# Output product to feed-forward of a two-layer backbone: VectorE's order written by hand, tiles in another assignment to halves

## The chip, the cores and the metric

The kernel runs on one core of a Trainium2 chip. Its time is the device time of one execution in microseconds; three executions of the kernel before are given, and one further execution was taken with a hardware profile.

## The reference

One inference step of two layers on 1024 sample tokens and 128 prompt tokens of width 1024, in float32. Each layer is a mixer (layer 0: a diagonal state-space scan beside a Fourier mixer; layer 1: pooling beside a gated MLP) and a squared-ReLU feed-forward, each between two RMS norms with a shift, scale and gate computed from the condition:

```python
def rmsnorm(x, g):
    xf = x.astype(F32)
    y = xf * lax.rsqrt(jnp.mean(xf * xf, axis=-1, keepdims=True) + EPS)
    return (y * g.astype(F32)).astype(x.dtype)

def run_layer(x, cond, mixer, ...):
    sh1, sc1, gt1, sh2, sc2, gt2 = modulation(cond, w_mod, b_mod)
    h = rmsnorm(x, g_mix_pre) * (1.0 + sc1) + sh1
    y, aux = mixer(h)                       # its last step is a product with w_out (1024 x 1024)
    x = x + gt1 * rmsnorm(y, g_mix_post)
    h = rmsnorm(x, g_ff_pre) * (1.0 + sc2) + sh2
    x = x + gt2 * rmsnorm(jnp.square(jax.nn.relu(h @ w1)) @ w2, g_ff_post)
```

The stage of this case lies between the mixer's product with w_out and the first product of the feed-forward with w1 (1024 x 4096).

## The kernel before

Tokens lie in nine tiles of 128: tiles 0 to 7 are the sample, tile 8 the prompt. A float32 operand of a product is split into a high and a low part in a rounded format (ScalarE writes the high part with a Copy, VectorE the low part with a subtraction), and each product is three matmuls: high by high, high by low, low by high.

`mixer_out` (L777) makes the product with w_out for one tile and one half of the 512 output columns at a time: `mm_tm` issues 24 matmuls (L252 to L254) into a PSUM bank `po`, of which there are three in turn. The activations of tiles 0 to 2, 3 to 5 and 6 to 8 are groups 0, 1 and 2, in the slots A0 to A15. The order is: first half of tiles 0, 1, 2, second half of the same, then both halves of 3, 8, 4, 5, 6, 7. The weights of the second half lie in W0 to W7. ScalarE copies `po` to `y` (L797; slots Y0, Y1 and E in turn); after a tile's second half `add_normed` (L674) takes the norm (`rms_scales`, L180), multiplies by the gate row `gt` (slot T, L688), adds the residual `xr` loaded by SP (L694), stores the sum, takes the next norm and scales (L699). `raw_tile` (L723) transposes the tile on TensorE (L731) and converts the blocks with scale and shift into the four quarters `raw` of one half j of the tokens (slots R0 to R7): tiles 0 to 3 and half of the prompt are half 0, tiles 4 to 7 half 1. Four of a tile's eight blocks are converted by ScalarE (L746) and four by VectorE (L744); tile 8 takes 32 small steps of ScalarE (L737).

`factors` (L749) then makes, for each half j, the seven right-hand factors x of a fast (seven-product) form of the feed-forward's first product: four sums of quarters (L766 to L773) and seven splits into a high part on ScalarE (L758, L761) and a low part on VectorE (L759, L762). They go to the slots that the table `XQ` lists. Names such as x14l in the profile are half 1, factor 4, low part.

`ff_up` (L808) runs 16 weight pairs. For a pair it makes seven weight factors (L841 on ScalarE, L842 and the sums L850 to L858 on VectorE), runs seven products of 12 matmuls a half (L96 to L98, 288 columns, in the banks puA, puB, puC) and turns them into hidden blocks (L893 to L915). The first pair runs half 0 through all seven products (1, 2, 6, 5, 7, 3, 4) and then half 1; the others run both halves product by product. In layer 0, jobs that compute modulation vectors (L126, with weights `mst` loaded to slot E and to staging slots) follow the pairs one by one.

The program's text gives dependencies and a priority; the order on each engine is set at build time by a planner that issues, engine by engine, what its model holds ready, earlier text first. `tc.manual_schedule(engines=...)` keeps the instructions of the named engines in the order of the text; the kernel before uses it for SP's DMA queue in the first stage.

The last stage (`ff_down`, L958) finishes tiles with the same `add_normed`, in layer 1 in the order 2, 3, 6, 7, 8, 0, 1, 4, 5; `layer1_mixer` (L1125) gates its three groups in the order 0, 1, 2.

Of the kernel before, what the change touches and what calls it, by code (L numbers as in the profile page):

```python
# [9 lines left out]
F32 = mybir.dt.float32  # L10
# [169 lines left out]
def rms_scales(K, ys):  # L180

    nc, v = K.nc, K.nc.vector
    n = len(ys)
    t = K.small.tile([128, 6, 3], F32, name="rms", tag="rms", bufs=4)
    for i, y in enumerate(ys):
        junk = K.small.tile([128, D], BF16, name="junk", tag="junk", bufs=1)
        nc.scalar.activation(junk, y, AF.Square, accum_out=t[:, 0, i:i + 1])
    t = t[:, :, :n]
    v.tensor_scalar(t[:, 1], t[:, 0], 1.0 / D, EPS, op0=ALU.mult, op1=ALU.add)
    nc.scalar.activation(t[:, 2], t[:, 1], AF.Sqrt)  # L190
    v.reciprocal(t[:, 3], t[:, 2])
    v.tensor_tensor(t[:, 4], t[:, 3], t[:, 3], op=ALU.mult)
    v.tensor_tensor(t[:, 4], t[:, 4], t[:, 1], op=ALU.mult)
    v.tensor_scalar(t[:, 4], t[:, 4], -0.5, 1.5, op0=ALU.mult, op1=ALU.add)
    v.tensor_tensor(t[:, 5], t[:, 3], t[:, 4], op=ALU.mult)
# [61 lines left out]
def build(tc, A):  # L257
# [6 lines left out]
    with ExitStack() as top:  # L264
# [20 lines left out]
        K.csil = csil  # L285
        K.xs = tc.dram_tile([D, D], F32, name="xs")
# [423 lines left out]


XQ = {}
for _ks, _ns in (([(j, i, p) for i in (1, 2) for j in (0, 1) for p in "hl"], [f"A{n}" for n in range(8)]),
                 ([(0, 6, "h"), (0, 6, "l"), (1, 6, "h"), (0, 5, "h"), (0, 5, "l"), (0, 7, "h"), (0, 7, "l"), (0, 3, "h")],
                  [f"A{n}" for n in range(8, 16)]),
                 ([(0, 3, "l"), (0, 4, "h"), (0, 4, "l")], ["W0", "W1", "W2"]),
                 ([(1, 6, "l"), (1, 5, "h"), (1, 5, "l")], ["Y0", "Y1", "T"]),
                 ([(1, 7, "h"), (1, 7, "l"), (1, 3, "h"), (1, 3, "l")], ["R0", "R1", "R2", "R3"]),
                 ([(1, 4, "h"), (1, 4, "l")], ["R5", "R7"])):
    XQ.update(zip(_ks, _ns))  # L720


def raw_tile(K, t, y, raw, scale, shift):  # L723
# [3 lines left out]
    v = nc.vector  # L727
    for kh in range(2):
# [3 lines left out]
        for k in range(4):  # L732
            kb = 4 * kh + k
            if t == 8:
                for j in range(2):
                    for b in range(2):
                        nc.scalar.activation(raw[j][2 * kh + b][:, k, 256:288],  # L737
                                             ps[:, 128 * k + 64 * j + 32 * b:128 * k + 64 * j + 32 * b + 32],
# [38 lines left out]
def mixer_out(K, layer, acts):  # L777
# [14 lines left out]
    for t, h in [(t, h) for h in range(2) for t in range(3)] + [(t, h) for t in (3, 8, 4, 5, 6, 7) for h in range(2)]:  # L792
        if h == 0:
            y[t] = yp.tile([128, D], F32, "y")
# [962 lines left out]
```

## Time and profile before

| | us |
|---|---|
| three executions | 2440.43, 2440.82 (median), 2446.5 |
| the profiled execution | 2445.58 |
| span of the profile | 2443.8 |
| TensorE busy (matmul) | 2276.6 (93%) |
| VectorE busy | 1715.2 (70%) |
| ScalarE busy | 986.1 (40%) |
| GpSimd busy | 193.4 (8%) |
| layer 0: output products, then the feed-forward's first pair | 488.3 to 592.5, 592.5 to 655.5 |
| layer 1: end of the output products to the end of the first pair | 1680.6 to 1738.4 |

Times in the rows are microseconds from the start of the span unless marked ns. PE is TensorE (PEld its weight loads), DVE VectorE, ACT ScalarE, POOL GpSimd, SPq the DMA queue that SyncE issues. L694 is line 694 of the kernel. [...]

### The profile page before, as it was taken

How to read it: one execution, taken by the hardware profiler on the slowest of the kernel's cores; microseconds unless marked ns; L12 is line 12 of the kernel's file. 1: busy time of each engine (PE TensorE's matmuls, PEld its weight loads, DVE VectorE, ACT ScalarE, POOL GpSimd, SP SyncE). 2: the span in 40 equal slices, each digit the busy share in tenths (PEclk: the TensorE clock that was granted, in tenths of full speed). 3: DMA queues.
4: the chain of work that ended last, by engine and by line, in shares of the span. 5: the costliest groups of instructions: out<-in, count | busy, mean ns of one | idle time of the engine just before them, and what ended most of it. 6: DMA issues, size and time to landing. Idle time of an engine off the chain costs nothing.

```text
span 2443.8 us, 34950 instructions
## 1 busy us (share of the span) xinstructions
PE 2276.6 (93%) x13462; PEld 1983.6 (81%) x13462; DVE 1715.2 (70%) x2800; ACT 986.1 (40%) x1712; POOL 193.4 (8%) x196
## 2 busy tenths in 40 slices
PE   7997775998799999999999799998899999999996
PEld 4996543987688889988888599887899999888884
DVE  7888998646665555756768944877765567567779
ACT  4543334546332233454333452446433334543332
POOL 0126863200000000000000000000000000000000
PEclk9998887999999999999999899998999999999998
DMA  8375573322456554644433431131344446444334
GB/s 316 132 247 184 187 271 114 128 79 86 135 184 222 183 168 133 234 155 139 127 113 101 170 123 40 61 112 67 115 145 128 131 144 229 149 141 127 122 102 172
DMA packets 200455, 361.50 MB, mean 148 GB/s; under 512 B 50064, under 2 KB 95760, under 8 KB 198240
## 3 DMA queue, kind: packets, MB, share of 16 engines
q1 hardware_dynamic: 200288, 359.26, 44.6%
q8 instruction: 106, 1.74, 0.3%
q14 instruction: 61, 0.50, 0.1%
HBM read 256.69 MB, written 102.51 MB: 147 GB/s over the span
## 4 chain that ended last, share of the span: by engine, by line
PE 76%; DVE 16%; ACT 3%; DMA 2%; issue 2%; POOL 1%; SPq 0%; DVEq 0%; ACTq 0%
PE pz L1060 7%; PE pz L1058 7%; PE pz L1059 7%; PE puA L96 6%; PE puA L97 5%; PE puA L98 5%; DVE tp L1559 3%; PE puC L96 3%; PE puC L98 3%; PE puC L97 3%; PE po L252 2%; PE po L253 2%; PE po L254 2%; PE pmod L126 2%; DVE xp L1566 1%
## 5 line engine op out<-in xcount | busy, mean ns | idle before, releaser
L1060 PE MATMUL pz<-wh,hl 128*128 128x512 f32 x840 | 324.8, 389 | 2.6 <-DVE hl L1053 2.6
L1059 PE MATMUL pz<-wl,hh 128*128 128x512 f32 x840 | 326.8, 389 | 0.0
L1058 PE MATMUL pz<-wh,hh 128*128 128x512 f32 x840 | 324.8, 389 | 0.0
L1052 ACT ACTIVATE hh<-hr 128x1024 fp32r<-128x1024 f32 x96 | 96.7, 1007 | 282.5 <-PE pz L1059 248.3
L1053 DVE TENSOR_TENSOR hl<-hr,hh 128x1024 fp32r<-128x1024 f32 x96 | 110.9, 1155 | 133.9 <-ACT hh L1052 133.8
L1060 PEld LDWEIGHTS pz<-wh,hl 128*128 128x128 f32 x840 | 157.7, 188 | 36.0 <-DVE hl L1053 3.4
L1058 PEld LDWEIGHTS pz<-wh,hh 128*128 128x128 f32 x840 | 157.7, 188 | 33.4 <-DVE z L1067 0.9
L1059 PEld LDWEIGHTS pz<-wl,hh 128*128 128x128 f32 x840 | 157.7, 188 | 32.6
L841 ACT ACTIVATE wh<-c 128x512 fp32r<-128x512 f32 x96 | 60.5, 630 | 187.9 <-DVE c L850 135.7
L897 DVE TENSOR_TENSOR h<-puA,c 128x576 f32<-128x576 f32 (+1 forms) x34 | 24.5, 722 | 154.3 <-PE puA L98 151.2
L253 PE MATMUL po<-wl,act 128*128 128x512 f32 x288 | 112.3, 390 | 0.0
L254 PE MATMUL po<-wh,act 128*128 128x512 f32 x288 | 112.2, 391 | 0.0
L252 PE MATMUL po<-wh,act 128*128 128x512 f32 x288 | 111.6, 392 | 0.0
L91 DVE TENSOR_TENSOR wl<-st,wh 128x1024 fp32r<-128x1024 f32 (+1 forms) x46 | 56.4, 1237 | 59.9 <-ACT wh L90 59.8
L842 DVE TENSOR_TENSOR wl<-c,wh 128x512 fp32r<-128x512 f32 x96 | 66.1, 689 | 34.5 <-ACT wh L841 34.1
L1559 DVE TENSOR_TENSOR tp<-rt,xp 128x1168 f32<-128x1168 f32 x48 | 80.5, 1715 | 11.7 <-ACT xp L1552 11.1
L841 ACT ACTIVATE wh<-st 128x512 fp32r<-128x512 f32 x96 | 57.2, 628 | 76.3 <-PE puB L97 29.0
L842 DVE TENSOR_TENSOR wl<-st,wh 128x512 fp32r<-128x512 f32 x96 | 63.7, 686 | 31.1 <-ACT wh L841 30.9
L126 PE MATMUL pmod<-mst,csil 128*32 128x512 f32 x384 | 77.7, 650 | 5.9 <-DMA mst<-in_w_mod_dram 4.4
L893 ACT ACTIVATE c<-puA 128x576 f32<-128x576 f32 (+1 forms) x68 | 42.2, 621 | 92.4 <-PE puA L98 91.3
L1031 DVE TENSOR_TENSOR wl<-u,wh 128x1024 fp32r<-128x1024 f32 x64 | 73.8, 1153 | 7.2 <-ACT wh L1030 7.2
L1031 DVE TENSOR_TENSOR wl<-raw,wh 128x1024 fp32r<-128x1024 f32 x64 | 73.1, 1153 | 4.2 <-ACT wh L1030 4.2
(493 smaller groups left out, 6848.3 us busy)
## 6 DMA issues: line engine op xcount, KB each, us to landing
hr<-hd SPq DMA_DIRECT2D x102, 512.0 KB
mst<-in_w_mod_dram SPq DMA_DIRECT2D x96, 512.0 KB
st<-in_w_ff_dram SPq DMA_DIRECT2D x68, 512.0 KB
hd<-hsum SPq DMA_DIRECT2D x120, 256.0 KB
raw<-in_w_ff_dram SPq DMA_DIRECT2D x56, 512.0 KB
hd<-h SPq DMA_DIRECT2D x98, 256.0 KB
ef<-ef SPq DMA_DIRECT2D x16, 1088.0 KB
xr<-xs SPq DMA_DIRECT2D x32, 512.0 KB
```

Source lines behind the costliest of these rows:

```text
L96: nc.tensor.matmul(ps, sh, mh, start=start, stop=False, skip_group_check=shared)
L97: nc.tensor.matmul(ps, sh, ml, start=False, stop=False, skip_group_check=shared)
L98: nc.tensor.matmul(ps, sl, mh, start=False, stop=stop, skip_group_check=shared)
L252: K.nc.tensor.matmul(ps, ah[kb][:, c], wh[:, s], start=kb == 0, stop=False)
L253: K.nc.tensor.matmul(ps, ah[kb][:, c], wl[:, s], start=False, stop=False)
L254: K.nc.tensor.matmul(ps, al[kb][:, c], wh[:, s], start=False, stop=kb == 7)
L842: v.tensor_tensor(wl, x, wh.bitcast(F32), op=ALU.subtract)
L1031: v.tensor_tensor(wl, w, wh.bitcast(F32), op=ALU.subtract)
L1058: nc.tensor.matmul(o, hh[:, q, t], wh[:, q], start=s == 0 and q == 0, stop=False)
L1059: nc.tensor.matmul(o, hh[:, q, t], wl[:, q], start=False, stop=False)
L1060: nc.tensor.matmul(o, hl[:, q, t], wh[:, q], start=False, stop=s == 1 and q == n - 1)
L1559: v.tensor_tensor(t[:, k], R[:, k:k + 1].to_broadcast([128, 2, 4, SC]), x, op=ALU.mult)
```

## The change

The tiles get new places: `PLACE` puts tiles 0, 1, 2 and 6 in half 0 and tiles 7, 3, 4 and 5 in half 1, and the order of the output products becomes: first halves of 0, 1, 2, second halves of 0, 1, 2, then 8, 6 and 7 whole, the first halves of 3, 4, 5 and last their second halves. `XQ` puts half 0's factors in A0 to A4 and A11 to A15 (groups 0 and 2), R1, R0, R3 and W0. VectorE's instructions of `mixer_out` stand in a `manual_schedule` block; `factors` becomes a list of steps (`factor_steps`) that `fill` puts at chosen places of that order, half 1's in two column parts. The gate product and the sum of squares are taken from PSUM half by half; tiles other than 5 are converted by ScalarE alone; tile 8 is converted whole to a staging tile and copied by GpSimd. The norm's inverse root is refined in another form, everywhere. Products 5 and 6 are exchanged for half 1 of the first pair, and layer 1's mixer takes its groups in the order 0, 2, 1, with two groups' slots exchanged.

```diff
 def rms_scales(K, ys):
     nc, v = K.nc, K.nc.vector
...
-        nc.scalar.activation(junk, y, AF.Square, accum_out=t[:, 0, i:i + 1])
+        nc.scalar.activation(junk, y, AF.Square, scale=0.5 / math.sqrt(D), accum_out=t[:, 0, i:i + 1])
     t = t[:, :, :n]
-    v.tensor_scalar(t[:, 1], t[:, 0], 1.0 / D, EPS, op0=ALU.mult, op1=ALU.add)
-    nc.scalar.activation(t[:, 2], t[:, 1], AF.Sqrt)
+    nc.scalar.activation(t[:, 2], t[:, 0], AF.Sqrt, bias=K.eps)
+    v.tensor_scalar(t[:, 1], t[:, 0], EPS / 4, None, op0=ALU.add)
     v.reciprocal(t[:, 3], t[:, 2])
-    v.tensor_tensor(t[:, 4], t[:, 3], t[:, 3], op=ALU.mult)
-    v.tensor_tensor(t[:, 4], t[:, 4], t[:, 1], op=ALU.mult)
-    v.tensor_scalar(t[:, 4], t[:, 4], -0.5, 1.5, op0=ALU.mult, op1=ALU.add)
-    v.tensor_tensor(t[:, 5], t[:, 3], t[:, 4], op=ALU.mult)
+    if n == 1:
+        v.scalar_tensor_tensor(t[:, 4], t[:, 1], t[:, 3], t[:, 2], op0=ALU.mult, op1=ALU.add)
+    else:
+        v.tensor_tensor(t[:, 4], t[:, 1], t[:, 3], op=ALU.mult)
+        v.tensor_tensor(t[:, 4], t[:, 4], t[:, 2], op=ALU.add)
+    v.reciprocal(t[:, 5], t[:, 4])
     return [t[:, 5, i:i + 1] for i in range(n)]
 
 
...
+        K.eps = K.const.tile([128, 1], F32, name="eps")
+        nc.gpsimd.memset(K.eps, EPS / 4)
...
+PLACE = {t: (n // 4, n % 4 // 2, n % 2) for n, t in enumerate((0, 1, 2, 6, 7, 3, 4, 5))}
...
+for _j, _ns in ((0, "A0 A1 A2 A3 A4 A11 A12 A13 A14 A15 R1 R0 R3 W0"),
+                (1, "A5 A6 A7 A8 A9 A10 W1 W2 Y0 Y1 T R2 R5 R7")):
+    XQ.update(zip([(_j, i, p) for i in (1, 2, 5, 6, 7, 3, 4) for p in "hl"], _ns.split()))
...
-def raw_tile(K, t, y, raw, scale, shift):
+def raw_tile(K, t, y, raw, scale, shift, both=False):
     nc = K.nc
     v = nc.vector
+    tmp = stage_tile(K, "praw")[:, :1024].rearrange("p (k n) -> p k n", k=8) if t == 8 else None
     for kh in range(2):
         ps = bank(K, "ptr", K.side_tags)
         for k in range(4):
             nc.tensor.transpose(ps[:, 128 * k:128 * k + 128], y[:, 512 * kh + 128 * k:512 * kh + 128 * k + 128], K.ident)
         for k in range(4):
             kb = 4 * kh + k
+            x = ps[:, 128 * k:128 * k + 128]
             if t == 8:
-                for j in range(2):
-                    for b in range(2):
-                        nc.scalar.activation(raw[j][2 * kh + b][:, k, 256:288],
-                                             ps[:, 128 * k + 64 * j + 32 * b:128 * k + 64 * j + 32 * b + 32],
-                                             AF.Identity, scale=scale[:, kb, 1:2], bias=shift[:, kb, 1:2])
+                nc.scalar.activation(tmp[:, kb], x, AF.Identity, scale=scale[:, kb, 1:2], bias=shift[:, kb, 1:2])
                 continue
-            o = raw[t // 4][2 * kh + t % 4 // 2][:, k, 128 * (t % 2):128 * (t % 2) + 128]
-            x = ps[:, 128 * k:128 * k + 128]
-            if k % 2:
+            j, half, b = PLACE[t]
+            o = raw[j][2 * kh + half][:, k, 128 * b:128 * b + 128]
+            if both and k % 2:
                 v.tensor_scalar(o, x, scale[:, kb, 0:1], shift[:, kb, 0:1], op0=ALU.mult, op1=ALU.add)
             else:
                 nc.scalar.activation(o, x, AF.Identity, scale=scale[:, kb, 0:1], bias=shift[:, kb, 0:1])
+        if t == 8:
+            for j in range(2):
+                for half in range(2):
+                    o = 64 * j + 32 * half
+                    nc.gpsimd.tensor_copy(raw[j][2 * kh + half][:, :, 256:288], tmp[:, 4 * kh:4 * kh + 4, o:o + 32])
-def factors(K, j, raw, xq):
...
+def factor_steps(K, j, raw, xq, parts):
+    def part(i, p, cols):
+        if (i, p) not in made:
+            made[i, p] = slot(K, XQ[j, i, p], [128, 4, 288], FR, f"x{j}{i}{p}")
+            if p == "l":
+                xq[j][i] = [made[i, "h"], made[i, "l"]]
+        return made[i, p][:, :, cols]
+    made = {}
+    def first(i, x, cols):
+        nc.scalar.activation(part(i, "h", cols), x[:, :, cols], AF.Copy, scale=-1.0 if i == 1 else 1.0)
+    def rest(i, x, cols):
+        h, l = (part(i, p, cols) for p in "hl")
         if i == 1:
+            v.scalar_tensor_tensor(l, x[:, :, cols], -1.0, h.bitcast(F32), op0=ALU.mult, op1=ALU.subtract)
         else:
+            v.tensor_tensor(l, x[:, :, cols], h.bitcast(F32), op=ALU.subtract)
+    def summed(x, y, op, cols):
+        v.tensor_tensor(x[:, :, cols], x[:, :, cols], y[:, :, cols], op=op)
+    whole = slice(0, 288)
+    steps = []
+    def step(*fs):
+        steps.append(lambda: [f[0](*f[1:]) for f in fs])
+    step((first, 1, b11, whole), (first, 2, b21, whole), (rest, 1, b11, whole))
+    if len(parts) > 1:
+        step((rest, 2, b21, whole))
+    for cols in parts:
+        step((summed, b11, b12, ALU.subtract, cols), (first, 5, b11, cols))
+        step((summed, b12, b22, ALU.subtract, cols), (first, 7, b12, cols))
+        step((rest, 5, b11, cols))
+        step((summed, b11, b22, ALU.add, cols), (first, 6, b11, cols))
+        step((rest, 7, b12, cols), (first, 3, b22, cols))
+        step((rest, 6, b11, cols))
+        step((summed, b21, b11, ALU.subtract, cols))
+        step((rest, 3, b22, cols))
+    if len(parts) == 1:
+        steps.insert(3, lambda: rest(2, b21, whole))
+    step((first, 4, b21, whole))
+    step((rest, 4, b21, whole))
+    return steps
...
-    for t, h in [(t, h) for h in range(2) for t in range(3)] + [(t, h) for t in (3, 8, 4, 5, 6, 7) for h in range(2)]:
+    y, sums = {}, {}
+    todo = []
+    def fill(n):
+        for _ in range(min(n, len(todo))):
+            todo.pop(0)()
+    def inverse(x, t, k):
+        v.reciprocal(t[:, k + 1], t[:, k])
+        v.scalar_tensor_tensor(t[:, k + 2], x, t[:, k + 1], t[:, k], op0=ALU.mult, op1=ALU.add)
+        v.reciprocal(t[:, k + 2], t[:, k + 2])
+        return t[:, k + 2]
+    def squares(x, out):
+        n = x.shape[1]
+        junk = K.small.tile([128, D], BF16, name="junk", tag="junk", bufs=1)
+        nc.scalar.activation(junk[:, :n], x, AF.Square, scale=0.5 / math.sqrt(D), accum_out=out)
+    def half_out(t, h):
         if h == 0:
             y[t] = yp.tile([128, D], F32, "y")
+            sums[t] = K.small.tile([128, 12, 1], F32, name="rms", tag="rms2", bufs=4)
+        g = gt
+        if t == 8:
+            if h == 0:
+                sums["g"] = norm_load(K, layer, 0, 1, stage_tile(K, "gt")[:, :D])
+            g = sums["g"]
+        s = sums[t]
+        c = slice(512 * h, 512 * h + 512)
         ps = bank(K, "po")
         mm_tm(K, t % 3, acts[t // 3], w[h], ps)
-        nc.scalar.activation(y[t][:, 512 * h:512 * h + 512], ps, AF.Copy)
-        if h == 1:
-            g = norm_load(K, layer, 0, 1, stage_tile(K, "gt")[:, :D]) if t == 8 else gt
-            add_normed(K, layer, 0, {int(t == 8): g}, [t], [y[t]])
-            raw_tile(K, t, y[t], raw, m["sc2"], m["sh2"])
+        squares(ps, s[:, h])
+        if h == 0:
+            nc.scalar.activation(s[:, 2], s[:, 0], AF.Identity, bias=K.eps)
+        v.tensor_tensor(y[t][:, c], ps, g[:, c], op=ALU.mult)
+    def normed(t, between=(1, 1, 0)):
+        s = sums[t]
+        xt = stage_tile(K, "xr")[:, :D]
+        if t == 8:
+            nc.sync.dma_start(xt, A["x_prompt"] if layer == 0 else K.xpd)
+        else:
+            nc.sync.dma_start(xt, K.xs[128 * t:128 * t + 128, :])
+        nc.scalar.activation(s[:, 4], s[:, 1], AF.Sqrt, bias=s[:, 2])
+        fill(between[0])
+        v.tensor_tensor(s[:, 3], s[:, 1], s[:, 2], op=ALU.add)
+        r = inverse(s[:, 3], s, 4)
+        v.scalar_tensor_tensor(y[t], y[t], r, xt, op0=ALU.mult, op1=ALU.add)
+        nc.sync.dma_start(K.xpd if t == 8 else K.xs[128 * t:128 * t + 128, :], y[t])
+        squares(y[t], s[:, 7])
+        nc.scalar.activation(s[:, 9], s[:, 7], AF.Sqrt, bias=K.eps)
+        fill(between[1])
+        v.tensor_scalar(s[:, 8], s[:, 7], EPS / 4, None, op0=ALU.add)
+        r = inverse(s[:, 8], s, 9)
+        v.tensor_scalar(y[t], y[t], r, None, op0=ALU.mult)
+        raw_tile(K, t, y[t], raw, m["sc2"], m["sh2"], t == 5)
+        fill(between[2])
     xq = [{}, {}]
-    for j in range(2):
-        factors(K, j, raw[j], xq)
+    with tc.manual_schedule(engines={v.engine}):
+        for h in range(2):
+            for t in range(3):
+                half_out(t, h)
+                if h:
+                    normed(t)
+        for t in (8, 6):
+            for h in range(2):
+                half_out(t, h)
+            normed(t)
+        todo += factor_steps(K, 0, raw[0], xq, [slice(0, 288)])
+        for h in range(2):
+            half_out(7, h)
+        normed(7, (1, 1, 1))
+        for t in (3, 4, 5):
+            half_out(t, 0)
+            fill(2 if t < 5 else 3)
+        last = todo.pop()
+        fill(99)
+        for t in (3, 4):
+            half_out(t, 1)
+            normed(t)
+        todo += factor_steps(K, 1, raw[1], xq, [slice(0, 128), slice(128, 288)])
+        half_out(5, 1)
+        todo.insert(2, last)
+        normed(5, (1, 2, 9))
+        fill(99)
     return xq
...
-            product("A", 6, False, js)
-            copied("A", 2)
-            product("C", 5, True, js)
-            copied("C", 5)
+            for i in (5, 6) if js == (1,) else (6, 5):
+                if i == 6:
+                    product("A", 6, False, js)
+                    copied("A", 2)
+                else:
+                    product("C", 5, True, js)
+                    copied("C", 5)
...
-            a, half, b = t // 4, t % 4 // 2, t % 2
+            a, half, b = PLACE.get(t, (0, 0, 0))
...
-          (("W0", "W1", "Y0", "Y1"), ("W2", "W3", "R2", "R3"), ("W4", "W5", "R4", "R5"))]
+          (("W0", "W1", "Y0", "Y1"), ("W4", "W5", "R4", "R5"), ("W2", "W3", "R2", "R3"))]
...
-        out = []
+        out = [None] * 3
-            mm = (m0, m1)[g % 2]
+            mm = (m0, m1)[g // 2]
-            vt2 = [slot(K, n, [128, 2, 4, 128], F32, "vt") for n in (("W6", "R0"), ("W7", "R1"))[g % 2]]
+            vt2 = [slot(K, n, [128, 2, 4, 128], F32, "vt") for n in (("W6", "R0"), ("W7", "R1"))[g // 2]]
...
-            out.append((ah, al))
+            out[g] = ah, al
-        for g in range(3):
-            nxt = values(g + 1) if g < 2 else None
+        for g in (0, 2, 1):
+            nxt = values({0: 2, 2: 1}[g]) if g != 1 else None
```

## Rows read from the trace of the kernel before

**Rows 1.** Busy time by stage: window, then each engine, TensorE's clock, DMA share, GB/s.

```profile
488.30:592.50 104.20, 104.02 (x484) 86.36 (x482) 50.83 (x133) 53.82 (x124) 0.00 (x0) 1.00 0.26 90
592.50:655.50 63.00, 43.87 (x257) 36.71 (x255) 51.64 (x96) 29.79 (x53) 0.00 (x0) 0.86 0.32 106
1680.60:1738.40 57.80, 42.81 (x241) 39.01 (x239) 50.47 (x90) 29.64 (x52) 0.00 (x0) 0.79 0.21 71
2370.00:2440.00 70.00, 50.40 (x220) 40.74 (x218) 69.32 (x133) 19.08 (x36) 0.00 (x0) 0.90 0.44 154
```

**Rows 2.** Timeline of TensorE, both layers: start, duration, engine, line, operation, operands.

```profile
592.37 0.29 PE L96 MATMUL puB<-x02h,wh 128*128 128x288 f32 x1
592.50 0.29 PE L97 MATMUL puB<-x02l,wh 128*128 128x288 f32 x1
...
655.17 0.29 PE L98 MATMUL puA<-x14h,wl 128*128 128x288 f32 x1
...
1738.11 0.29 PE L98 MATMUL puA<-x14h,wl 128*128 128x288 f32 x1
```

**Rows 3.** Waits of TensorE, layer 0's tail: total us, times, longest.

```profile
PE pmod L126 <- DMA mst<-in_w_mod_dram: 4.4, 2, 3.4
PE puC L98 <- DVE wl L842: 4.1, 2, 3.9
```

**Rows 4.** Timeline of VectorE and TensorE in layer 0's tail.

```profile
626.20 0.76 DVE L699 TENSOR_SCALAR y<-y,rms 128x1024 f32<-128x1024 f32 x1
...
630.32 1.12 PE L731 MATMUL ptr<-cst,y 128*128 128x128 f32 x8
...
633.23 1.35 DVE L766 TENSOR_TENSOR raw<-raw 128x1152 f32<-128x1152 f32 x1
...
646.02 1.36 DVE L762 TENSOR_TENSOR x14l<-raw,x14h 128x1152 fp32r<-128x1152 f32 x1 [1.78 <-ACT x14h L761]
```

**Rows 5.** Groups of VectorE by shape, last stage and layer 0's tail: busy us, mean ns.

```profile
L1067 DVE TENSOR_TENSOR zr<-pz,zr 128x512 f32<-128x512 f32 x12 | 7.7, 683 | 4.2 <-PE pz L1060 4.2
...
L1070 DVE TENSOR_TENSOR zr<-zr 128x512 f32<-128x512 f32 x8 | 5.2, 686 | 0.0
...
L898 DVE SCALAR_TENSOR_TENSOR h<-h 128x288 f32<-128x288 f32 x6 | 2.7, 455 | 0.1
...
L768 DVE TENSOR_TENSOR raw<-raw 128x1152 f32<-128x1152 f32 x2 | 2.7, 1348 | 0.0
```

**Rows 6.** Groups by shape, 488.3 to 592.5 us (output products of layer 0).

```profile
L187 ACT ACTIVATE junk<-y 128x1024 bf16<-128x1024 f32 x15 | 16.0, 1069 | 9.6 <-DVE y L694 9.3
...
L688 DVE TENSOR_TENSOR y<-y,gt 128x1024 f32<-128x1024 f32 x8 | 9.7, 1216 | 0.0
L694 DVE SCALAR_TENSOR_TENSOR y<-y,rms,xr 128x1024 f32<-128x1024 f32 x7 | 9.0, 1283 | 0.2
L737 ACT ACTIVATE raw<-ptr,mc,mc 128x32 f32<-128x32 f32 x32 | 8.7, 469 | 2.0 <-PE ptr L731 2.0
L746 ACT ACTIVATE raw<-ptr,mc,mc 128x128 f32<-128x128 f32 x20 | 8.6, 477 | 6.6 <-PE ptr L731 4.9 <-DVE raw L744 1.6
L744 DVE TENSOR_SCALAR raw<-ptr,mc,mc 128x128 f32<-128x128 f32 x20 | 7.6, 406 | 0.9 <-ACT raw L746 0.8
...
L699 DVE TENSOR_SCALAR y<-y,rms 128x1024 f32<-128x1024 f32 x6 | 4.5, 753 | 1.1 <-DMA xs<-y 0.8 <-DMA xpd<-y 0.2
L187 ACT ACTIVATION_READ_ACCUMULATOR junk<-y 128x1 f32 x15 | 3.1, 204 | 0.0
L190 ACT ACTIVATE rms<-rms 128x1 f32<-128x1 f32 x14 | 2.8, 198 | 2.1 <-DVE rms L189 1.9
...
L191 DVE RECIPROCAL rms<-rms 128x1 f32<-128x1 f32 x13 | 2.0, 157 | 1.2 <-ACT rms L190 1.2
```

**Rows 7.** Timeline of SP's DMA queue, first stage.

```profile
45.23 3.97 SPq L87 DMA_DIRECT2D st<-in_w_in_dram  x3
52.55 0.33 SPq L352 DMA_DIRECT2D x<-in_x_sample_dram  x1
```

## What the change should do to the time

> **What bounds the kernel now.** The first view to read is the table of busy time by stage [rows 1]. In layer 0's stretch of output products (488.3 to 592.5 us) TensorE is busy for 104.02 of 104.20 us at clock 1.00: nothing on another engine can shorten it. In the stretch behind it (592.5 to 655.5 us, until the feed-forward's first weight pair is through) TensorE is busy for 43.87 of 63.00 us at a mean clock of 0.86, while VectorE goes from 49% to 82% busy. Layer 1 has the same stretch from 1680.6 to 1738.4 us: 42.81 of 57.80 us, clock 0.79. So the time lies in the two tails, not in the products.
>
> How much lies there: in layer 0, 63.00 - 43.87 = 19.1 us idle, and the lost clock is at most (1 - 0.86) x 63.0 = 8.8 us: 27.9 us at most; what TensorE does there would take some 63.0 - 27.9 = 35.1 us at full speed. In layer 1, 15.0 us idle and (1 - 0.79) x 57.8 = 12.1 us: 27.1 us, with 30.7 us of work. Both layers together hold 55 us. Full speed is visible in the timeline: successive 288-column products start 0.13 us apart [rows 2], so the two halves of the first pair (168 products) are 22 us.
>
> The list of waits says what ends last in the tail: low-order weight parts of VectorE, 4.1 us; the load of modulation weights, 4.4 us [rows 3]. The timeline of the tail shows why VectorE is late [rows 4]. The last tile is normalised at 626.20 us, 34 us after the last product, because VectorE made the first half's factors and the weights in between; its transposes start at 630.32 us, behind products that TensorE had in its order ahead of them; the second half's factors then run from 633.23 to 647.4 us (14.2 us). The norms of tiles 6 and 7 and most factors of both halves come behind the last product.
>
> **The change, part by part.** T is the end of the last output product.
>
> *First half's factors ahead of T.* Tiles 0, 1, 2 and 6 now make the first half; their factors go to slots of groups 0 and 2, whose activations are done by then. A half is 11 VectorE steps of 1152 columns (seven low parts, four sums); ten of them come ahead of T, 10 x 1.35 us = 13.5 us [rows 5], spread over tile 7's two products and the first products of tiles 3 to 5. One product with its share of transposes takes 104.2 / 18 = 5.8 us [rows 1], so these five products are 29 us. VectorE's own tile work there is some 7 us, so the steps fit, and VectorE has 104.2 - 50.8 = 53 us idle under the products today. Cost: none while that cover holds; without it the 13.5 us return to the tail. The eleventh stays behind T (x04's low part, in W0, a slot of the output weights): 1.35 us.
>
> *The tile's chain.* The gate product moves from one step of 1.22 us to two of 0.68 us that read PSUM, and the sum of squares is taken from PSUM: no copy of the product any more. Per tile [rows 6]: square of half a row with its readout 0.7 + 0.2 (half of 1.07 to 1.07, plus 0.2), square root 0.2, four one-column steps 0.6, the residual step 1.28, square and readout 1.27, square root 0.2, four steps 0.6, scaling 0.75: 5.9 us, and 0.6 us of hops between engines by estimate: 6.5 us. TensorE takes 11.6 us for a tile's two products; only tiles 0 to 2 and 3 to 4 follow 5.8 us apart, and a product's bank is wanted again three products later. All eight conversions of a tile now lie on ScalarE (8 x 0.48 = 3.8 us), which frees 28 x 0.41 = 11 us of VectorE per layer [rows 6]. I take T as unmoved.
>
> [...] The 128x512 step that reads PSUM lasts 683 ns and the one that reads SBUF 686 ns [rows 5]: no difference. [...]
>
> *Tile 8.* 32 small ScalarE steps, 8.7 us in all [rows 6], become 8 of 0.48 us and 8 GpSimd copies; 5 us less of ScalarE per layer, ahead of T. GpSimd is idle here, and its copies are wanted only by the factors; 0.
>
> *Behind T.* Left are: tile 4's end and tile 5's whole chain. Tile 4's last product ends 5.8 us before T, so it is scaled at about T + 2 (6.5 us plus a wait behind tile 3's conversions). Tile 5: VectorE's gate step, x11's and x12's low parts and x04's (3 x 1.35, of which 2.5 us fill the ScalarE legs), and the 6.5 us chain with up to 3.8 us behind tile 4's conversions: 0.7 + 4.05 - 2.5 + 6.5 + 3.8, scaled at T + 12.5. Transposes 1 us, eight conversions on two engines 2 us: T + 15.5. Then two column parts (128 and 160 columns by four blocks): 8 steps of 512 columns, 0.69 us, and 8 of 640, on the line between 0.69 and 1.35 us 0.82 us, and x14's low part 1.35 us: 13.4 us, so T + 28.9. In between come VectorE's ten steps for the feed-forward's first hidden blocks, 10 x 0.46 = 4.6 us of which some 3 us fall in this chain: T + 31.9. The last product of the pair adds 1.6 us: T + 33.5. TensorE has meanwhile 35 us (layer 0) or 31 us (layer 1) of work at full speed, so it is near its own bound. Today the same points are T + 63.0 and T + 57.8: 28 us (to TensorE's 35) and 24 us less at best.
>
> [...] Bounds 0 and 12 us a layer; I take 7 and 5, nearer to the low end since the weights can be split while TensorE runs the last three products (slots of the first half's output weights are free 17 us ahead of T). **Layer 0: -21 us. Layer 1: -19 us.**
>
> *Outside this stage.* The shorter norm saves a ScalarE-VectorE round trip and one or two one-column steps, 0.16 us each, at nine tiles of the tail of the kernel, where VectorE is busy for 69.32 of 70.00 us [rows 1], and at six group norms: 0 to 4 us, 1.5 us taken. Tiles 3 and 7 now end late in the final stage and stand early in its order: 0 while VectorE is never idle there, up to 2 us if it is. The gating of groups in the order 0, 2, 1 delays one low part of group 0 to the end of the third group's products, wanted 5 us later: 0, at worst 5 us. Products 5 and 6 exchanged: 0.
>
> **Rivals.** *Half the gain* (order of TensorE): products that wait stand ahead of transposes that are ready, as today at 630.32 us, and VectorE's head waits in the chain of halves. Three holes of 4 us and one load: each layer gains 12 us: 2445.6 - 25 = 2421 us profiled, 2416 on the median. For it: the 4 us hole, in today's order that nobody wrote by hand. Against: fewer steps are left behind T.
>
> *No gain* (what is behind the hand-written order waits): if VectorE took no outside step until the sequence ends, the pair's 11 weight steps would start near T + 29, and the 28.7 us of products (168, and 48 of the next pair, at 0.13 us) would follow: T + 58 or later. Layer 1 gains nothing, layer 0 some 5 us; with the 1.5 us of norms 2439 us profiled, 2434 us on the median. The trace speaks against: the early SP sequence is written by hand in the same way, and loads of w_in that come later in the program stand inside it [rows 7]. [...]
>
> *Slower* (a tile's chain outgrows its products): if a tile's chain, with its four ScalarE legs each behind the previous tile's 3.8 us of conversions, lasts longer than 11.6 us, the gate steps come late, banks are not free, and TensorE waits at each of 9 tiles. At 6.5 + 2 x 3.8 = 14.1 us it is still 2.5 us a tile, 45 us over two layers, half of them at a lower clock, say 55 us, against 42 us gained: 2441 + 13 = 2454 us on the median. Deciding point: 11.6 us. Against: only one leg can meet those conversions at a tile's pace.
>
> **How the numbers follow.** 2445.6 - 21 - 19 - 1.5 = 2404.1 us against the profiled execution's 2445.6 us (its span is 2443.8). The median of the runs is 4.8 us below that execution; the same saving off 2440.8 us gives **2399 us**. Chances: forecast (2385 to 2411 us) 0.60; half the gain (2411 to 2432) 0.21; no gain 0.07; slower 0.07; better than the forecast, down to TensorE's own bound, 0.05. The low end, 2385 us, is the best case of both layers (28 + 24 us) and 4 us of norms; the high end, 2430 us, takes in the half gain. About 0.3% (7 us) is what a measurement can tell from no change. The first two cases and the fifth are faster by more, 0.86; no gain lies within it but for a hundredth: same 0.06, slower 0.08.
>
> **What would show it.** Right: products 488 to 592 us unchanged and busy throughout; low parts of x01 to x03 ahead of T; the first pair done at T + 39 (layer 1) and T + 42 (layer 0) instead of 58 and 63; TensorE's clock above 0.9 in both tails. Wrong: TensorE idle between output products with VectorE's gate step as releaser (slower); weight steps of the first pair behind x14's low part (no gain); transposes of tile 5 over 3 us behind its scaling (half).

## The result, and the profile after

The changed kernel takes 2461.90 us (median of four runs, 2456.35 to 2463.65) against 2440.62 us for the kernel before on the same chip: ratio 1.0078, 95% interval 1.0056 to 1.0100. It is 21 us slower where 2399 us had been forecast. The profiled execution took 2463.65 us, its span is 2461.9 us.

The table of busy time by stage, changed kernel (window; then busy time and instructions of each engine; TensorE's granted clock as a share of full speed, DMA share, GB/s). The stretches are cut as in [rows 1]: output products, then up to the end of the first pair, in each layer.

```profile
487.30:605.30 118.00, 109.94 (x501) 90.04 (x500) 55.61 (x114) 60.07 (x147) 2.06 (x8) 0.97 0.24 84
605.30:651.90 46.60, 38.55 (x237) 33.40 (x236) 37.79 (x67) 23.35 (x47) 0.00 (x0) 0.89 0.40 132
1569.70:1710.90 141.20, 119.89 (x535) 98.44 (x533) 81.00 (x178) 66.31 (x159) 2.00 (x8) 0.92 0.27 94
1710.90:1754.30 43.40, 34.69 (x221) 32.09 (x220) 37.83 (x67) 22.85 (x48) 0.00 (x0) 0.92 0.24 81
```

Both tails are shorter, as forecast: 46.6 us for 63.0 and 43.4 us for 57.8 [rows 1]. But TensorE, busy for 104.02 of 104.20 us under layer 0's products before, now waits there, and layer 1's products, 107.3 us before, take 141.2 us. The same view of the kernel before, layer 1's products:

```profile
1573.30:1680.60 107.30, 107.30 (x516) 89.82 (x515) 74.90 (x200) 59.47 (x137) 0.00 (x0) 1.00 0.34 117
```

The profile's group of the first of the three matmuls shows the total wait (behind the second bar; first the kernel before, then the changed one), and the waits of TensorE in layer 0's and then layer 1's products show the pieces (waited for: us in all, times, longest):

```profile
L252 PE MATMUL po<-wh,act 128*128 128x512 f32 x288 | 111.6, 392 | 0.0
...
L255 PE MATMUL po<-wh,act 128*128 128x512 f32 x288 | 116.8, 408 | 22.1 <-DVE y L860 22.1
```

```profile
PE po L255 <- DVE y L860: 7.4, 5, 3.9
PE ptr L736 <- DVE y L881: 0.7, 1, 0.7
...
PE po L255 <- DVE y L860: 14.7, 6, 7.3
PE psv L1347 <- DVE vt L1344: 5.9, 1, 5.9
```

L860 is the gate step, which takes a product out of its bank. All runs in one table, in us from the profiled executions: products from the first matmul of the output product to the end of the last (T), tail from T to the end of x14's last product, and the rest from there to the end of the span. Medians and ratios are of the timed runs.

| kernel | products 0 | tail 0 | products 1 | tail 1 | rest | median | ratio to before (95%) |
|---|---|---|---|---|---|---|---|
| before | 104.1 | 62.9 | 107.3 | 57.8 | 705.4 | 2440.6 to 2441.4 | 1 |
| changed | 118.0 | 46.5 | 141.2 | 43.4 | 707.6 | 2461.9 | 1.0078 (1.0056 to 1.0100) |
| e1 banks in turn | 103.6 | 46.4 | 126.9 | 44.7 | 706.7 | 2440.1 | 0.9991 (0.9978 to 1.0003) |
| e2 gate row early | 118.5 | 46.8 | 125.2 | 42.7 | 707.4 | 2444.3 | 1.0017 (1.0006 to 1.0027) |
| e3 both | 103.6 | 48.6 | 109.4 | 49.6 | 708.9 | 2427.7 | 0.9945 (0.9934 to 0.9957) |
| e4 no hand order | 115.1 | 41.1 | 137.8 | 41.4 | 708.5 | 2454.7 | 1.0049 (1.0034 to 1.0064) |
| e5 both, no hand order | 103.6 | 43.9 | 108.2 | 41.1 | 705.4 | 2416.5 | 0.9904 (0.9890 to 0.9918) |
| e6 e3, last stage's order | 103.6 | 47.4 | 109.4 | 49.1 | 707.5 | 2425.3 | 0.9939 (0.9926 to 0.9953) |
| e7 changed, with a copy | 105.6 | 52.3 | 113.3 | 53.3 | 707.8 | 2435.6 | 0.9988 (0.9975 to 1.0000) |
| e8 before, banks in turn | 103.6 | 53.7 | 107.3 | 55.9 | 705.3 | 2431.1 | 0.9965 (0.9952 to 0.9977) |
| e9 e5, last stage's order | 103.6 | 43.7 | 108.2 | 41.1 | 705.0 | 2414.1 | 0.9878 (0.9860 to 0.9897) |
| e10 e9, two engines convert | 103.6 | 42.6 | 108.1 | 45.0 | 705.1 | 2416.8 | 0.9891 (0.9873 to 0.9909) |
| e11 e5, old slots | 103.6 | 48.6 | 108.2 | 47.1 | 706.4 | 2419.2 | 0.9908 (0.9893 to 0.9923) |
| e12 e9, with a copy | 103.6 | 44.6 | 107.5 | 50.1 | 707.0 | 2424.0 | 0.9932 (0.9919 to 0.9946) |

From the span before (2443.8) to the one after (2461.9): products +13.9 and +33.8, tails -16.4 and -14.4, rest +2.2, start of the stage -1.2; the stretch between the layers is 917.8 us in both. The tails gave 31 of the 40 us forecast; the products took 48. The waits listed above are 8.1 of the 13.9 us and 21.3 of the 33.8. For the rest TensorE is busy for longer: its granted clock in these stretches is 0.97 and 0.92 where it was 1.00, and 12 matmuls of the first pair now stand among the output products of each layer.

No variant's edit touches what runs ahead of layer 0's stage, and still that stage starts between 482.6 and 491.8 us in the profiled executions. So the stretches are a surer measure than the totals, and 2 or 3 us between two medians are no finding by themselves.

**Where TensorE's time goes in layer 0.** `bank` hands out a bank by a counter that the transposes advance too: each tile's second half is followed by two transposes, so 0b, 1b, 2b and 8a (a and b are the halves) stand three counts apart and fall on the same bank of three: the products do not take the banks in turn, as the account of the kernel before has it. The planner then lets TensorE run what has another bank. The order of first matmuls in the built programs (the changed kernel's is the same in both layers; of 6b only 2 of 24 matmuls stand ahead of 1b, the others behind it):

```
TensorE, before (layer 0)    0a 1a 2a 0b 3b 1b 8b 2b 8a 3a 4b 4a 5b 5a 6b 7b 6a 7a
TensorE, changed             0a 1a 2a 0b 8b 6b 1b 2b 8a 7b 6a 4a 7a 5a 3a 3b 4b 5b
VectorE, changed             0a 1a 2a 0b 1b 2b 8a 8b 6a 6b 7a 7b 3a 4a 5a 3b 4b 5b
```

The changed kernel's gate steps stand in another order than its products. In the timeline (start, duration, engine, line, operation, idle before and releaser) the fifth and sixth gate steps, of 1b and 2b, wait for their squares, and these for TensorE, which had been sent to 8b and 6b:

```profile
520.64 0.60 ACT L842 ACTIVATE junk<-po 128x512 bf16<-128x512 f32 x1 [5.56 <-PE po L257]
521.36 0.69 DVE L860 TENSOR_TENSOR y<-po,gt 128x512 f32<-128x512 f32 x1 [4.05 <-ACT junk L842]
...
531.97 0.60 ACT L842 ACTIVATE junk<-po 128x512 bf16<-128x512 f32 x1 [6.16 <-PE po L257]
532.69 0.69 DVE L860 TENSOR_TENSOR y<-po,gt 128x512 f32<-128x512 f32 x1 [5.25 <-ACT junk L842]
533.43 0.50 PE L255 MATMUL po<-wh,act 128*128 128x512 f32 x1 [0.63 <-DVE y L860]
```

The gate step of 8b starts at 540.83 us, 31.7 us after TensorE began that product (509.1). With two banks held like that (by 8b, and by 6b until 554.0 us), the third goes round alone: product, square, gate step, next product. The gate step runs behind the square, not beside it (square 520.64 to 521.24, its readout from 521.13, gate step 521.36): each of the 36 gate steps starts at least 0.12 us after the square of its bank has ended, and 31 of them carry a wait on ScalarE of their own in the built program. What two readers side by side would do was not tried. So a bank that a 0.6 us copy freed is now freed by two steps of 0.6 and 0.7 us on two engines, each in its own queue.

**In layer 1** a second cause is added. The gate row lies in slot T, where the mixer's spatial gating keeps its products to the end:

```profile
1593.13 5.46 PE L1347 MATMUL psv<-misc,vt 128*128 128x128 f32 x24 [5.91 <-DVE vt L1344]
...
1599.46 0.68 DVE L1350 TENSOR_TENSOR svt<-psv,misc 128x512 f32<-128x512 f32 x1
1599.57 1.72 SPq L675 DMA_DIRECT2D gt<-gate  x2
...
1605.09 1.89 DVE L860 TENSOR_TENSOR y<-po,gt 128x512 f32<-128x512 f32 x3 [1.93 <-DMA gt<-gate]
1605.92 0.76 PE L255 MATMUL po<-wh,act 128*128 128x512 f32 x1 [7.33 <-DVE y L860]
```

Three products fill the banks by 1587.2 us; their gate steps start at 1605.09, when the row is there. TensorE, which used to have products to do under the third group's gating, waits 5.9 us for the gating and 7.3 us for banks. Behind these waits its granted clock is 0.50 (1606 to 1612 us), and 1.00 from 1614 us on. Before, the row was wanted only behind a tile's second half.

### The profile page after: what moved, and what is told of

It is laid out like the page before. It is cut to its first block, busy times and chain, and to the rows that moved or that the text cites. A ratio compares the mean times of both kernels' runs of the same rounds, so it can differ in the third digit from the quotient of the medians.

```text
span 2461.9 us, 34894 instructions
## 1 busy us (share of the span) xinstructions
PE 2278.0 (93%) x13462; PEld 1983.3 (81%) x13462; DVE 1697.1 (69%) x2679; ACT 987.6 (40%) x1746; POOL 199.7 (8%) x213
## 5 line engine op out<-in xcount | busy, mean ns | idle before, releaser
L255 PE MATMUL po<-wh,act 128*128 128x512 f32 x288 | 116.8, 408 | 22.1 <-DVE y L860 22.1
L256 PE MATMUL po<-wl,act 128*128 128x512 f32 x288 | 115.1, 401 | 0.0
L257 PE MATMUL po<-wh,act 128*128 128x512 f32 x288 | 114.1, 399 | 0.0
L255 PEld LDWEIGHTS po<-wh,act 128*128 128x128 f32 x288 | 55.9, 194 | 36.4 <-DVE y L860 17.2
```

Source lines behind the costliest of these rows:

```text
L255: K.nc.tensor.matmul(ps, ah[kb][:, c], wh[:, s], start=kb == 0, stop=False)
L256: K.nc.tensor.matmul(ps, ah[kb][:, c], wl[:, s], start=False, stop=False)
L257: K.nc.tensor.matmul(ps, al[kb][:, c], wh[:, s], start=False, stop=kb == 7)
```

## The experiments

**e1 to e4: what holds the banks.**

e1, banks in turn, and e2, the gate row early (e3 is both, e4 replaces the `manual_schedule` block by `if True:`):

```diff
+    turn = list(range(K.turn, K.turn + 18))
...
-        ps = bank(K, "po")
+        tag, bufs = K.bank_tags[turn.pop(0) % 3]
+        ps = K.psum.tile([128, 512], F32, name="po", tag=tag, bufs=bufs)
```

```diff
-        svt = Slots(K, "T")
+        svt = Slots(K, "E", "E", "R1")
```

> The changed kernel, and the 18 output products of a layer take the three banks strictly in turn (before, transposes advanced the same counter, so that 0b, 1b, 2b and 8a all fell on one bank, and TensorE ran 8b and 6b ahead of 1b in the other two). Theory A (two of three banks are held by products that TensorE takes early and VectorE's hand-written order reads late): TensorE's waits for the gate step between output products fall from 7.4 us in layer 0 to under 1 us, T moves from 605 to about 593 us, layer 1's stretch loses some 14 of its 34 extra us; 2461.9 - 13 - 14 = 2435 us, 0.998 of the kernel before. Rival B (the square stands behind conversions in ScalarE's queue, and the gate step behind the square): banks in turn do not shorten that, waits stay above 5 us and the time within 4 us of 2462. Rival C (the two low parts or sums that the hand order puts between gate steps of tiles 3 to 5): only the 5.3 us wait at 584 us and its neighbour stay; 2450 us.

Measured: 2440.1 us, products of layer 0 in 103.6 us, no wait for banks left there, layer 1's products 14.3 us shorter. Theory A holds. Rivals B and C fall: ScalarE's queue and the steps between the gates of tiles 3 to 5 are as before, and the waits are gone. In the built program TensorE's order is now VectorE's.

> The changed kernel, and layer 1's spatial gating keeps its product in slots E, E and R1 instead of T, so that the gate row (slot T) can be loaded some 30 us before the first output product of layer 1 instead of behind the last gated group. Layer 0 is the same as in the changed kernel. Theory D (in layer 1 the first three gate steps wait for a row whose slot the mixer still holds): the first gate step of layer 1 starts near 1580 us instead of 1605, the 7.3 us wait and most of the 5.9 us wait for the gating go, and the half clock behind them: 13 to 18 us less, 2446 us. Rival (the products only wait elsewhere, for the third group's low parts at 1603 us or for banks out of turn): at most 4 us, 2458 us.

Measured: 2444.3 us; layer 0 unchanged at 118.5 us, layer 1's products 16.0 us shorter. Theory D holds.

> Both edits together. If A and D are two separate causes, their gains add: 2461.9 - 13 - 14 - 15 = 2420 us, 0.991 of the kernel before, with T in layer 0 near 593 us and the stretch of layer 1's output products near 107 us as in the kernel before. If they are one cause seen twice (TensorE out of banks), the sum is less by the smaller of the two: 2433 us. If B holds, 2445 us or more.

Measured: 2427.7 us. Single gains 21.9 and 17.6 us, together 34.3: two causes, as the products show (103.6 and 109.4 us). The 5 us short of the sum lie in the tails, which are 2.1 and 6.2 us longer than in the changed kernel.

> The changed kernel without the hand-written order: VectorE's instructions in this stage are placed by the planner like those of the other engines. TensorE's product order stays 0b, 8b, 6b, 1b. Theory A: VectorE then reads 8b and 6b where TensorE makes them, layer 0's waits between products go (about 13 us), layer 1 keeps its late gate row (15 us), and the factors of the first half come later again (the tails lose some 5 us a layer of what they gained): 2455 us, with T in layer 0 near 593 us. Rival B (ScalarE's queue and two readers of a bank): waits for the gate step stay at several us in layer 0, T stays above 600 us, 2465 us or more.

Measured: 2454.7 us, the number that theory A gave, but not for its reason: the products still take 115.1 and 137.8 us (T was to fall to 593 and is 606). The hand order is not what makes TensorE wait: without it 7.2 of the 8.1 us of waits stay in layer 0, and VectorE's gate steps stand in the same order in the built program, because (argued, not tried) y of tile 8 has the slot of y of tile 0. Of what e4 gains in the profiled execution, 6.3 us lie in the products and 7.4 in the tails (41.1 and 41.4 us).

**e5: the hand order where banks are in turn.** e3 with `if True:` in place of the `manual_schedule` block.

> Banks in turn and the early gate row as before, and VectorE's hand-written order taken out, so that the planner places its instructions. In the kernel without the order the pair was done at T + 41 in both layers, in the one with banks, row and order at T + 49 to 50. Theory H (once TensorE has its banks, the hand order itself costs in the tails, since the gate step and the chain stand behind weight and factor steps in an order fixed by the text): T stays near 594 and 1671 us, the pair is done near T + 41, 2427.6 - 7 - 8 = 2413 us. Rival (the order is what brings the first half's factors ahead of T; without it they slide behind T again): T + 50 or later, 2428 us or more.

Measured: 2416.5 us, 11 us faster than with the order. Theory H holds (tails of 43.9 and 41.1 us; layer 0's is 3 us over). The timeline of VectorE in layer 1's tail shows why, first e3, then e5. L883 scales tile 5, L746 converts it, L783 are sums: 512 columns are the part that needs tiles 7 and 3 only, 640 the part with tile 5.

```profile
1691.42 0.76 DVE L883 TENSOR_SCALAR y<-y,rms 128x1024 f32<-128x1024 f32 x1
1695.41 1.29 DVE L952 TENSOR_TENSOR wl<-st,wh 128x512 fp32r<-128x512 f32 x2 [3.24 <-ACT wh L951]
...
1699.18 0.41 DVE L746 TENSOR_SCALAR raw<-ptr,mc,mc 128x128 f32<-128x128 f32 x1 [0.53 <-ACT raw L748]
1699.51 1.41 DVE L783 TENSOR_TENSOR raw<-raw 128x512 f32<-128x512 f32 x2
...
1704.91 1.75 DVE L783 TENSOR_TENSOR raw<-raw 128x640 f32<-128x640 f32 x2
...
1711.99 1.36 DVE L780 TENSOR_TENSOR x14l<-raw,x14h 128x1152 fp32r<-128x1152 f32 x1 [0.64 <-ACT x14h L773]
```

```profile
1677.75 0.68 DVE L783 TENSOR_TENSOR raw<-raw 128x512 f32<-128x512 f32 x1
...
1686.14 0.69 DVE L780 TENSOR_TENSOR x16l<-raw,x16h 128x512 fp32r<-128x512 f32 x1
...
1686.94 0.75 DVE L883 TENSOR_SCALAR y<-y,rms 128x1024 f32<-128x1024 f32 x1
...
1690.50 0.73 DVE L746 TENSOR_SCALAR raw<-ptr,mc,mc 128x128 f32<-128x128 f32 x2
1691.14 1.75 DVE L783 TENSOR_TENSOR raw<-raw 128x640 f32<-128x640 f32 x2
...
1697.99 1.36 DVE L780 TENSOR_TENSOR x14l<-raw,x14h 128x1152 fp32r<-128x1152 f32 x1 [0.53 <-ACT x14h L773]
```

The hand order puts the first column part behind tile 5's conversions, though VectorE idles for 3.24 us ahead of them: 12.5 us from there to x14's low part. The planner does that part while tile 5's norm is on its way, and 6.9 us remain.

**e6 and e9: the last stage's order.** e3 and e5 with

```diff
-    ... ((2,), (3,), (6,), (7,), (8,), (0,), (1,), (4,), (5,)):
+    ... ((2,), (6,), (4,), (5,), (8,), (0,), (1,), (7,), (3,)):
```

> Banks in turn and early gate row, with the hand order, and the last stage takes its tiles in the order 2, 6, 4, 5, 8, 0, 1, 7, 3 in place of 2, 3, 6, 7, 8, 0, 1, 4, 5: under the new places of the tiles these are again the four tiles of the second quarter first and the four of the first quarter, which wait for the last of the seven products, behind them. From the end of layer 1's first pair to the end of the span the kernel before takes 705.4 us, the changed one 707.6, banks and row 708.9. Theory E (the moved places make the last stage wait for sums it wanted later): 2 to 3 us less, 2425 us. Rival (VectorE is never idle there, so the order does not matter): within 1 us of 2427.6.

> Banks in turn, early gate row, planner's order of VectorE, and the last stage in the order 2, 6, 4, 5, 8, 0, 1, 7, 3. If the last stage's order is worth by itself what it showed under the hand order (2427.6 to 2425.3), the sum is 2416.5 - 2.3 = 2414 us, 0.989 of the kernel before. If that difference was only scatter between runs, 2416 to 2417 us.

Measured: 2425.3 and 2414.1 us, 2.3 and 2.4 us under their neighbours with intervals that overlap. The rest of the span is 707.5 us for 708.9, and 705.0 us for 705.4. Theory E is not shown: e5 has 705.4 us with the changed order, as the kernel before. e9 is the fastest kernel here, 1.2% ahead of the kernel before.

**e7 and e12: a copy frees the bank.** The changed kernel, and e9, with

```diff
-        squares(ps, s[:, h])
+        nc.scalar.activation(y[t][:, c], ps, AF.Copy)
+        squares(y[t][:, c], s[:, h])
...
-        v.tensor_tensor(y[t][:, c], ps, g[:, c], op=ALU.mult)
+        v.tensor_tensor(y[t][:, c], y[t][:, c], g[:, c], op=ALU.mult)
```

> The changed kernel, and ScalarE copies each output product from its bank to y as in the kernel before; the square and the gate product read y. One short reader per bank instead of two one after the other, of which the second stands in VectorE's order; banks still out of turn, gate row still late. Theory A in its narrow form (it is how long a product holds its bank that counts): no wait for banks in layer 0, T near 593 us, layer 1's stretch near 110 us since a copy needs no gate row: 2461.9 - 13 - 30 = 2419 us. Wider form (TensorE's order 0b, 8b, 6b, 1b against VectorE's 0b, 1b, 2b, 8a delays every tile even with free banks): T near 593 us but the last tile later, 2435 us. Rival B (ScalarE's queue is too full to serve a bank in time): one more step of 0.6 us per product makes it worse, 2465 us.

Measured: 2435.6 us, as the wider form of theory A has it. The products fall to 105.6 and 113.3 us without any change of banks or row, so it is the time for which a product holds its bank that makes TensorE wait (in layer 1 the copy also takes away the wait for the gate row). But the products still stand out of order (0b, 8b, 1b, 6b in layer 0), tile 4 is scaled at T + 13.9 us in both layers (e1: T + 4.2 and 4.5), and the tails are 52.3 and 53.3 us. That this order makes tile 4 late is the forecast's reason and fits; ScalarE's 36 more steps are a rival that was not separated from it.

> The kernel of e9 (banks in turn, early gate row, planner's order, last stage's order), and each output product is copied from its bank by ScalarE first; square and gate product read the copy. With banks in turn no product waits for a bank (T - start of the products is 103.6 us in layer 0 there), so a bank that is free 0.8 us earlier brings nothing, while ScalarE has 36 steps of 0.6 us more and the chain of the last tile gets about 0.6 us longer: 2414 to 2418 us. Rival (two readers in turn still cost the chain: the gate step waits for the square and its readout at each product): 3 us or more faster, 2411 us or less.

Measured: 2424.0 us, 10 us slower than e9 and outside what either side gave. Layer 0's tail is 0.9 us longer, layer 1's 9.0 us: there tile 4 is scaled at T + 20.2 us (e9: T + 5.7) in the order that the planner then makes, and the granted clock of that tail is 0.83 (e9: 1.00). How much of the loss is the copy and how much the planner's new order is not separated.

**e8: the kernel before with banks in turn.** The edit of e1 in the kernel before.

> The kernel before, and its output products take the three banks in turn; nothing else. TensorE is busy for 104.02 of 104.20 us there already with banks out of turn, since a copy frees each bank at once. Theory A: no change, within 3 us of the kernel before. Rival (the turn of the banks is a gain of its own, whatever reads them, and e1 measured that): 10 us or more faster.

Measured: 2431.1 us, 10 us faster: theory A failed and the rival's number came, though not under the products. These are no faster (103.6 and 107.3 us); the tails are, by 9.2 and 1.9 us. Before, 6b and 7b stood ahead of 6a and 7a in layer 0, so two tiles were finished by the last two products; in turn, tile 6 is complete two products ahead of T. That fits layer 1, where 6a stood ahead of 7b before too and little is gained. But it is argued, not tried, and not all: layer 0's last three tiles (5, 6, 7) are scaled at T - 2.7, + 20.6, + 27.6 us for T + 12.4, + 26.3, + 34.4, and tile 5, which moves most, was complete four products ahead of T in both kernels; the planner's order on VectorE changed as well. Against this kernel the rest of the change (e5) is worth 14.6 us.

**e10: conversions on two engines, and e11: the old slots.** e9 with `t != 8` for `t == 5` in the call of `raw_tile`; e5 with the `XQ` table of the kernel before.

> The kernel of the run before, and all sample tiles are converted half by ScalarE and half by VectorE (as tile 5 is, and as in the kernel before) instead of by ScalarE alone. Rival B in the tail (the last products' squares and the chain of tile 5 stand behind conversions in ScalarE's queue: tile 5 is scaled at T + 21 there where T + 12.5 was forecast): the chain gets some 1.4 us shorter for each of tiles 4 and 5, 2 to 5 us less in both layers, 2410 us. Other way (both engines reading one bank take turns, and VectorE has its steps of the factors to do): no gain or up to 4 us slower, 2414 to 2418 us.

Measured: 2416.8 us, intervals overlapping with e9's: no gain (layer 0's tail 1.1 us shorter, layer 1's 3.9 us longer). Whether the conversions set the end, or what VectorE takes on in exchange, this does not separate. In the tails ScalarE's conversions wait for VectorE's for up to 0.82 us (layer 0) and 1.49 us (layer 1).

> Banks in turn, early gate row, planner's order, the last stage as in the changed kernel (the kernel of 2416.5 us), and the factors go to the slots of the table of the kernel before: half 0's factors 6, 5, 7 and 3 then lie in slots that the activations of tiles 3 to 5 or 6 to 8 hold, partly until T. Theory F (the gain that is left comes from half 0's factors lying ahead of T, for which the slots of finished groups are needed): x06's and x05's low parts and what follows slide behind T, the pair is done near T + 50 instead of T + 41 to 44, 2416.5 + 14 = 2430 us, that is the time of the kernel before with banks in turn (2431). Rival (VectorE's time behind T is not what ends last; order of tiles and the shorter chain make the gain): within 4 us of 2416.5.

Measured: 2419.2 us, within the rival's 4 us, while the tails of the profiled execution are 4.7 and 6.0 us longer (it is the slowest of e11's six; e5's is the fastest of its four). The low parts of x02, x06, x03 and x04 slid (in layer 0 x02 to 591.0 us for 555.5, x06 to 595.6 for 577.3), but only x06's and x04's to behind T, by 0.6 and 2.6 us; x05's and x07's stayed some 20 us ahead of T. So what theory F needs hardly came about, and it stays open.

## Why the prediction was wrong, point by point

**"I take T as unmoved."** This is the step that failed: T moved by 13.9 us in layer 0 and 33.8 us in layer 1. The argument held a tile's chain of 6.5 us against the 11.6 us of its two products and let a bank be wanted "again three products later". The chain was near enough (its terms add up to 6.4 us, not 6.5): from the end of its last product to the end of its scaling it took 8.0, 7.3 and 7.8 us for tiles 0 to 2 (509.3 to 517.3, 520.1 to 527.4, 531.9 to 539.7), with 0.2 to 0.8 us for the store of y, whose row [rows 6] had shown and the sum had left out. No run shows the 0.6 us of hops between engines in that sum: in the chain of tile 0 a step on the next engine starts 0.02 to 0.03 us after the one that it waits for. The banks were not in turn. That stood in the code (one counter for products and transposes) and in the built order of the kernel before (3b ahead of 1b); the prediction took the text's order for TensorE's.

**The gate product.** It was costed by its duration (0.68 us; 0.69 us in the changed kernel) and as "no copy any more". Not costed: whom the step waits for (the square of the same bank, and in layer 1 a row in a slot that is still in use), and that TensorE waits for it in turn (7.4 and 14.7 us). A copy waits for neither (before, ScalarE's idle time ahead of the copies, 47.9 us in 20 waits, ends with TensorE's product each time); e7 gives back 26 us with nothing but the copy.

**The rival "slower"** had the right place and the right sign to look for (TensorE idle between products, gate step as releaser, some 2454 us), at a chance of 0.07. Its own condition, a chain of over 11.6 us behind conversions, never came true.

**Behind T** the sum came out near, in part by luck. In the changed kernel tile 5 was scaled at T + 13.5 and 14.1 us (T + 12.5 forecast), converted at T + 18.2 and 20.4 (T + 15.5), and the pair was done at T + 46.5 and 43.4 (T + 42 and 39). But T was late there, and the waits ahead of it left the chains of tiles 3 and 4 time (argued, not tried). Where T is unmoved, tile 5 is scaled at T + 21.1 and 21.4 us in e5, and in e3, with the hand order, at T + 17.9 and 21.3: the chain of the last tiles was forecast 5 to 9 us too short. In e5 the tails of 43.9 and 41.1 us still lie 2 us from the forecast, since from tile 5's scaling to the end of x14's low part 13.4 and 11.7 us passed where 19.4 had been forecast; the planner had done the first column part by then. Two misses cancel. No run shows the 7 and 5 us taken off a layer as such: in e5 TensorE idles for 6.62 and 6.28 us of the tails at a granted clock of 1.00, in the changed kernel for 8.05 and 8.71 us at 0.89 and 0.92; its wait for the load of modulation weights is 2.0 us there (4.4 before). With that, e5 and e9 at 2414 to 2417 us lie within the range of 2385 to 2430; the tails gain 19 and 17 us for 21 and 19.

**First half's factors.** Seen as forecast: x03's low part stands at 1693.39 us, 17.5 us ahead of T in layer 1 (with T earlier, in e3, 9.7 us). What they are worth alone is open (e11).

**No gain and half gain.** The planner places outside steps inside the hand order (three weight steps of layer 1's first pair, 1714.53 to 1715.73 us, stand between two steps of tile 5's norm), so the first did not occur. The second named VectorE's waits in the order, and e3 against e5 shows them: 11 us.

**Outside the stage.** 1.5 us from the shorter norm is not seen: the rest is 705.4 us in e5 as before.

## What to carry to other kernels

Before the reader of a PSUM bank is changed, write down for each bank who releases it, behind what in which queue, and which product takes it next by the built order, not by the text; a short copy that waits for nothing may be worth more than the steps it costs (26 us in e7), as long as the banks do not go round in turn (in e12, where they do, it gained nothing). A counter shared by two kinds of tiles can undo a rotation (21.9 us in e1). An order fixed by hand on one engine should be held against the planner's own once the other causes are out: here it cost 11 us.

## What the runs showed that was not expected

An idle stretch cost twice here, with the same work. In e3's tail of layer 0 TensorE waits for 1.19 and 1.82 us, and its products then start 0.24 us apart, as far as 612.2 us, where they are 0.13 us apart before and after. That is some 2.5 us more for some 23 matmuls, on top of the 3.0 us of waiting:

```profile
604.29 0.40 PE L96 MATMUL puB<-x12h,wh 128*128 128x288 f32 x1 [1.19 <-ACT x12h L773]
606.50 0.61 PE L96 MATMUL puC<-x03h,wh 128*128 128x288 f32 x1 [1.82 <-ACT wh L951]
...
607.15 0.44 PE L96 MATMUL puA<-x07h,wh 128*128 128x288 f32 x1
607.39 0.44 PE L97 MATMUL puA<-x07l,wh 128*128 128x288 f32 x1
...
612.40 0.30 PE L98 MATMUL puB<-x12h,wl 128*128 128x288 f32 x1
612.53 0.29 PE L98 MATMUL puC<-x03h,wl 128*128 128x288 f32 x1
```

The granted clock of the tails tells the same, e3 and then e5 (windows of layer 0's and layer 1's tail): 0.89 and 0.86 with the hand order, 1.00 and 1.00 without, for as much work. These are single executions: e6, with e3's order in this stage, has 0.93 and 0.90, and e9, with e5's, 0.96 and 1.00.

```profile
594.00:642.60 48.60, 40.83 (x256) 35.85 (x254) 39.31 (x72) 27.11 (x59) 0.00 (x0) 0.89 0.42 136
1670.90:1720.50 49.60, 36.82 (x240) 35.13 (x239) 40.69 (x74) 28.61 (x60) 0.00 (x0) 0.86 0.24 82
```

```profile
594.70:638.50 43.80, 37.18 (x256) 32.01 (x254) 37.39 (x71) 27.46 (x59) 0.00 (x0) 1.00 0.46 153
1666.30:1707.40 41.10, 34.82 (x241) 31.54 (x239) 37.36 (x71) 27.61 (x60) 0.00 (x0) 1.00 0.29 99
```
